# RMSNorm with row repetition: six of eight tiles compute their squares and sums four rows at a time

## The chip, the cores and the metric

The kernel runs on one core of a Trainium2 chip. The metric is the time of one execution on the device, in microseconds (us). The profile is of one such execution.

## The reference

```python
B, S, D = 8, 512, 2048
x_rep = np.repeat(x, 2, axis=1)
rms = np.sqrt((x_rep ** 2).mean(axis=-1, keepdims=True) + 1e-6)
out = (x_rep / rms * gamma[None, None, :]).astype(np.float32)
```

There are 4,096 rows of 2,048 float32 numbers. Each row is divided by its root mean square, multiplied by gamma, and written out twice, one copy after the other. 33.6 MB are read and 67.1 MB written.

## The kernel before

The rows are cut into eight tiles. A tile has 128 partitions with K = 4 rows each, so a load brings 4 MB and a store takes 8 MB. The buffer `y` of a tile has K * R = 8 row places in each partition, since each row is written twice (R = 2). The load puts the four input rows into places 4 to 7. `scale` for row k reads place 4 + k and writes the scaled row to place 2k, and `repeat` copies the even places to the odd ones. So the whole output tile is built in the buffer that held the input. The pool `rows` holds three such buffers: the load of tile i must wait until the store of tile i - 3 has landed.

The work of a tile, in `compute`, is row by row. ScalarE squares a row and sums it in the same instruction (`square`, L64, with an accumulator that a second, short instruction reads out), and takes the root of the mean (L68). The squared row itself is not used and goes to a scratch tile `sq` in PSUM. VectorE takes the reciprocal (L73) and multiplies the row by it and by gamma in one instruction (L74). After the four rows ScalarE copies places 0 and 2 to 1 and 3, and VectorE copies 4 and 6 to 5 and 7 (both L81, 128x4096).

The order on each engine is the program's own (`manual_schedule`): an engine takes its instructions in the order in which they are written, and waits at each until what it needs is there. On ScalarE the copy of tile i therefore stands ahead of the first square of tile i + 1.

All loads (L52) and stores (L56) of the tiles are issued from SP, and so go into one queue in one written order: loads 0 (in two halves), 1, 2; stores 0, 1, 2; loads 3, 4, 5; stores 3, 4; loads 6, 7; stores 5, 6, 7. A load or store that waits on SP holds back everything behind it. Gamma comes through ScalarE's queue (L95) and is spread over the partitions by GpSimd (L96) before the first scale.

```python
loads_after = {2: (3, 4, 5), 4: (6, 7)}
for i in range(ntiles):
    compute(i)
    store(i, 0, K)
    for j in loads_after.get(i, ()):
        load(j, nc.sync)
```

Of the kernel before, what the change touches and what calls it, by code (L numbers as in the profile page):

```python
# [1 line left out]

# [4 lines left out]


@with_exitstack
def kernel(  # L10
    ctx: ExitStack,
    tc: tile.TileContext,
    x: bass.AP,
    gamma: bass.AP,
    out: bass.AP,
):
    nc = tc.nc
    P = nc.NUM_PARTITIONS
    f32 = mybir.dt.float32
    Act = mybir.ActivationFunctionType  # L20
    Alu = mybir.AluOpType

    B, S, D = x.shape
    Bo, So, Do = out.shape
    R = So // S
    assert R == 2 and D == Do and B == Bo and So == S * R
    eps = 1e-6
    inv_d = 1.0 / float(D)


    K = 4
    N = B * S
    assert N % (P * K) == 0
    ntiles = N // (P * K)
    x_t = x.rearrange("b s d -> (b s) d").rearrange("(n p k) d -> n p k d", p=P, k=K)
    out_t = out.rearrange("b s d -> (b s) d").rearrange("(n p j) d -> n p (j d)", p=P, j=K * R)

    singles = ctx.enter_context(tc.tile_pool(name="singles", bufs=1))
    rows = ctx.enter_context(tc.tile_pool(name="rows", bufs=3))
    junk = ctx.enter_context(tc.tile_pool(name="junk", bufs=1, space=bass.MemoryType.PSUM))  # L40
    small = ctx.enter_context(tc.tile_pool(name="small", bufs=8))

    ys = []

    def load(i, eng, parts=1):


        y = rows.tile([P, K * R, D], f32, name="y")
        step = K // parts
        for k in range(0, K, step):  # L50
            at = K * (R - 1) + k
            eng.dma_start(out=y[:, at : at + step, :], in_=x_t[i, :, k : k + step, :])  # L52
        ys.append(y)

    def store(i, k0, k1):
        nc.sync.dma_start(  # L56
            out=out_t[i, :, R * k0 * D : R * k1 * D],
            in_=ys[i][:, R * k0 : R * k1, :].rearrange("p j d -> p (j d)"),
        )

    def square(i, k):
        sq = junk.tile([P, D], f32, name="sq")
        ss = small.tile([P, 1], f32, name="ss")
        nc.scalar.activation(  # L64
            out=sq[:], in_=ys[i][:, K * (R - 1) + k, :], func=Act.Square, accum_out=ss[:]
        )
        rms = small.tile([P, 1], f32, name="rms")
        nc.scalar.activation(out=rms[:], in_=ss[:], func=Act.Sqrt, scale=inv_d, bias=eps_t[:])  # L68
        return rms

    def scale(i, k, rms):
        rstd = small.tile([P, 1], f32, name="rstd")
        nc.vector.reciprocal(out=rstd[:], in_=rms[:])  # L73
        nc.vector.scalar_tensor_tensor(  # L74
            out=ys[i][:, R * k, :], in0=ys[i][:, K * (R - 1) + k, :], scalar=rstd[:], in1=gamma_b[:],
            op0=Alu.mult, op1=Alu.mult,
        )

    def repeat(i, k0, k1, copy):
        y_r = ys[i].rearrange("p (k r) d -> p k r d", r=R)  # L80
        copy(out=y_r[:, k0:k1, 1, :], in_=y_r[:, k0:k1, 0, :])  # L81

    def compute(i):
        for k in range(K):
            scale(i, k, square(i, k))
        repeat(i, 0, K // 2, nc.scalar.copy)
        repeat(i, K // 2, K, nc.vector.tensor_copy)


    ctx.enter_context(tc.manual_schedule())  # L90
    load(0, nc.sync, parts=2)
    gamma_b = singles.tile([P, D], f32, name="gamma_b")
    cuts = [0, *range(D // 4, D + 1, D // 8)]
    for c0, c1 in zip(cuts, cuts[1:]):
        nc.scalar.dma_start(out=gamma_b[0:1, c0:c1], in_=gamma[c0:c1].partition_broadcast(1))  # L95
    nc.gpsimd.partition_broadcast(out_ap=gamma_b[:], in_ap=gamma_b[0:1, :])  # L96
    eps_t = singles.tile([P, 1], f32, name="eps_t")
    nc.vector.memset(eps_t, eps)  # L98
    load(1, nc.sync)
    load(2, nc.sync)  # L100

    assert ntiles == 8
# [8 lines that stand above are left out]
# [1 line left out]
_INS = ['x', 'gamma']  # L114
_OUTS = [((8, 1024, 2048), 'float32')]


# [23 lines left out]
```

## Time and profile before

| | |
|---|---|
| median of 3 runs | 239.7 us (239.38 to 240.03) |
| the profiled execution's own time | 239.72 us |
| its span in the trace | 237.9 us |
| ScalarE busy | 101.0 us, 106 instructions |
| VectorE busy | 96.5 us, 73 instructions |
| bytes moved, mean rate over the span | 100.69 MB, 423 GB/s |

The own time is 1.8 us longer than the span, which begins and ends with the core's instructions. In the rows of the profile's costliest groups, a row gives the line, the engine, the operation, what is written and read, the number of instructions, then after the first bar the busy time of all of them in us and the mean of one in ns, and after the second bar how long the engine was idle just before them and what ended most of that. In the timeline a line gives the start in us, the length in us, and the instruction. A transfer has its issue in the timeline of SP (a third of a us); its data moves later, and its landing is seen where something that waited for it goes on.

### The profile page before, as it was taken

What the parts mean: (1) busy time and instruction counts of PE and PEld (TensorE: products, weight loads), DVE (VectorE), ACT (ScalarE), POOL (GpSimd) and SP (SyncE); (2) the same over time, 40 slices, a digit from 0 to 9 for tenths busy, and PEclk for the clock granted to TensorE, in tenths of its full rate; (3) what the DMA queues carried; (4) which work ended last, traced back from release to release, by engine and by line L of the source; (5) the groups of instructions that cost most, each with busy time, mean ns of one, the idle gap of its engine ahead of it and who ended that gap; (6) DMA issues with size and microseconds to landing.
All of it is one profiled execution on the core that took longest, in us unless ns stands there. A gap on an engine that the chain in (4) does not pass through costs nothing.

```text
span 237.9 us, 287 instructions
## 1 busy us (share of the span) xinstructions
DVE 96.5 (41%) x73; ACT 101.0 (42%) x106; POOL 2.5 (1%) x5
## 2 busy tenths in 40 slices
DVE  0049999960000000059999960000199990000000
ACT  2697999900000000099999920000599960000000
POOL 0030000000000000000000000000000000000000
DMA  7999998989899998999998999989998989999994
GB/s 265 436 446 441 441 441 353 530 353 496 386 452 430 397 485 353 441 441 441 441 518 364 464 419 430 452 369 430 435 518 364 518 364 485 397 452 430 408 474 176
DMA packets 2464, 100.69 MB, mean 423 GB/s; under 512 B 279, under 2 KB 285, under 8 KB 286
## 3 DMA queue, kind: packets, MB, share of 16 engines
q1 hardware_dynamic: 2448, 100.66, 98.5%
q14 instruction: 2, 0.02, 0.0%
q10 hardware_dynamic: 14, 0.01, 0.0%
HBM read 33.56 MB, written 67.11 MB: 423 GB/s over the span
## 4 chain that ended last, share of the span: by engine, by line
DMA 58%; ACT 12%; DVE 9%; issue 1%; POOLq 1%; ACTq 1%; SPq 0%
DMA y<-in_x_dram 33%; DMA out_dram<-y 21%; ACT sq L64 8%; DVE y L74 7%; DMA gamma_b<-in_gamma_dram 4%; ACT y L81 3%; DVE y L81 2%; ACT rms L68 1%; POOLq L136 1%; ACTq L95 1%; DVE rstd L73 0%; POOLq L96 0%; SPq L56 0%
## 5 line engine op out<-in xcount | busy, mean ns | idle before, releaser
L64 ACT ACTIVATE sq<-y 128x2048 f32<-128x2048 f32 x32 | 59.7, 1865 | 87.8 <-DMA y<-in_x_dram 87.8
L74 DVE SCALAR_TENSOR_TENSOR y<-y,rstd,gamma_b 128x2048 f32<-128x2048 f32 x32 | 75.3, 2352 | 4.1 <-POOL gamma_b L96 3.0
L73 DVE RECIPROCAL rstd<-rms 128x1 f32<-128x1 f32 x32 | 5.0, 158 | 94.6 <-ACT rms L68 94.3
L81 ACT COPY y<-y 128x4096 f32<-128x4096 f32 x8 | 28.7, 3590 | 1.4 <-DVE y L74 1.4
L81 DVE COPY y<-y 128x4096 f32<-128x4096 f32 x8 | 18.3, 2294 | 0.3
L68 ACT ACTIVATE rms<-ss,eps_t 128x1 f32<-128x1 f32 x32 | 9.4, 295 | 1.0
L64 ACT ACTIVATION_READ_ACCUMULATOR sq<-y 128x1 f32 x32 | 6.0, 187 | 0.0
L64 ACT ACT_TABLE_LOAD x1 | 1.3, 1283 | 3.0 <-issue 3.0
L96 POOL PARTITION_BROADCAST gamma_b<-gamma_b x1 | 2.3, 2294 | 12.2 <-DMA y<-in_x_dram 12.2
L68 ACT ACT_TABLE_LOAD x1 | 1.3, 1283 | 0.0
L98 DVE MEMSET eps_t<- 128x1 f32 x1 | 0.1, 59 | 0.8 <-PEq L125 0.8
L125 POOL MEMSET const-uint8-127<- 128x1 uint8 x1 | 0.1, 102 | 0.0
L125 POOL MEMSET const-bfloat16-1.0<- 128x1 bf16 x1 | 0.1, 101 | 0.0
L125 POOL MEMSET const-float32-0.0<- 128x1 f32 x1 | 0.1, 98 | 0.2 <-issue 0.2
L125 POOL MEMSET const-float32-1.0<- 128x1 f32 x1 | 0.1, 98 | 0.0
## 6 DMA issues: line engine op xcount, KB each, us to landing
y<-in_x_dram SPq DMA_DIRECT2D x7, 4096.0 KB, 14.6
y<-in_x_dram SPq DMA_DIRECT2D x2, 2048.0 KB, 7.4
out_dram<-y SPq DMA_DIRECT2D x8, 24.4
gamma_b<-in_gamma_dram ACTq DMA_DIRECT2D x6, 1.0 KB
gamma_b<-in_gamma_dram ACTq DMA_DIRECT2D x1, 2.0 KB
```

Of the source, the lines that this page charges most:

```text
L64: nc.scalar.activation(out=sq[:], in_=ys[i][:, K * (R - 1) + k, :], func=Act.Square, accum_out=ss[:])
L68: nc.scalar.activation(out=rms[:], in_=ss[:], func=Act.Sqrt, scale=inv_d, bias=eps_t[:])
L73: nc.vector.reciprocal(out=rstd[:], in_=rms[:])
L74: nc.vector.scalar_tensor_tensor(out=ys[i][:, R * k, :], in0=ys[i][:, K * (R - 1) + k, :], scalar=rstd[:], in1=gamma_b[:], op0=Alu.mult, o ...
L81: copy(out=y_r[:, k0:k1, 1, :], in_=y_r[:, k0:k1, 0, :])
L95: nc.scalar.dma_start(out=gamma_b[0:1, c0:c1], in_=gamma[c0:c1].partition_broadcast(1))
L96: nc.gpsimd.partition_broadcast(out_ap=gamma_b[:], in_ap=gamma_b[0:1, :])
L98: nc.vector.memset(eps_t, eps)
L125: nc = _bacc.Bacc("TRN2", target_bir_lowering=False, num_devices=1)
L136: with _tile.TileContext(nc) as tc:
```

## The change

Tiles 0 and 3, which the change's own words call tight, keep the work row by row. For tiles 1, 2, 4, 5, 6 and 7 the new function `scale_wide` squares all four rows in one ScalarE instruction of 128x8192. Its output goes to places 0 to 3 of the tile's own buffer. VectorE sums it with one `tensor_reduce` to four sums a partition; ScalarE takes the four roots in one instruction; VectorE takes the four reciprocals in one, and then scales row by row. `scale` no longer takes the reciprocal itself: for tiles 0 and 3 that instruction has moved into `compute`, just ahead of the call. `repeat`, the loads, the stores and their order stay as they were.

```diff
@@ -68,11 +68,9 @@
         nc.scalar.activation(out=rms[:], in_=ss[:], func=Act.Sqrt, scale=inv_d, bias=eps_t[:])
         return rms
 
-    def scale(i, k, rms):
-        rstd = small.tile([P, 1], f32, name="rstd")
-        nc.vector.reciprocal(out=rstd[:], in_=rms[:])
+    def scale(i, k, rstd):
         nc.vector.scalar_tensor_tensor(
-            out=ys[i][:, R * k, :], in0=ys[i][:, K * (R - 1) + k, :], scalar=rstd[:], in1=gamma_b[:],
+            out=ys[i][:, R * k, :], in0=ys[i][:, K * (R - 1) + k, :], scalar=rstd, in1=gamma_b[:],
             op0=Alu.mult, op1=Alu.mult,
         )
 
@@ -80,9 +78,29 @@
         y_r = ys[i].rearrange("p (k r) d -> p k r d", r=R)
         copy(out=y_r[:, k0:k1, 1, :], in_=y_r[:, k0:k1, 0, :])
 
+    def scale_wide(i):
+
+        nc.scalar.activation(out=ys[i][:, :K, :], in_=ys[i][:, K * (R - 1) :, :], func=Act.Square)
+        ss = small.tile([P, K], f32, name="ss_w")
+        nc.vector.tensor_reduce(
+            out=ss[:], in_=ys[i][:, :K, :], op=Alu.add, axis=mybir.AxisListType.X
+        )
+        rstd = small.tile([P, K], f32, name="rstd_w")
+        nc.scalar.activation(out=rstd[:], in_=ss[:], func=Act.Sqrt, scale=inv_d, bias=eps_t[:])
+        nc.vector.reciprocal(out=rstd[:], in_=rstd[:])
+        for k in range(K):
+            scale(i, k, rstd[:, k : k + 1])
+
     def compute(i):
-        for k in range(K):
-            scale(i, k, square(i, k))
+
+        if i in (0, 3):
+            for k in range(K):
+                rms = square(i, k)
+                rstd = small.tile([P, 1], f32, name="rstd")
+                nc.vector.reciprocal(out=rstd[:], in_=rms[:])
+                scale(i, k, rstd[:])
+        else:
+            scale_wide(i)
         repeat(i, 0, K // 2, nc.scalar.copy)
         repeat(i, K // 2, K, nc.vector.tensor_copy)
```

## The prediction

> **What bounds the kernel now.** I read the page first: busy share of the DMA engines, DMA queues, then the price rows.
>
> ```profile
> DMA  7999998989899998999998999989998989999994
> ...
> q1 hardware_dynamic: 2448, 100.66, 98.5%
> ...
> L64 ACT ACTIVATE sq<-y 128x2048 f32<-128x2048 f32 x32 | 59.7, 1865 | 87.8 <-DMA y<-in_x_dram 87.8
> L74 DVE SCALAR_TENSOR_TENSOR y<-y,rstd,gamma_b 128x2048 f32<-128x2048 f32 x32 | 75.3, 2352 | 4.1 <-POOL gamma_b L96 3.0
> L73 DVE RECIPROCAL rstd<-rms 128x1 f32<-128x1 f32 x32 | 5.0, 158 | 94.6 <-ACT rms L68 94.3
> L81 ACT COPY y<-y 128x4096 f32<-128x4096 f32 x8 | 28.7, 3590 | 1.4 <-DVE y L74 1.4
> L81 DVE COPY y<-y 128x4096 f32<-128x4096 f32 x8 | 18.3, 2294 | 0.3
> L68 ACT ACTIVATE rms<-ss,eps_t 128x1 f32<-128x1 f32 x32 | 9.4, 295 | 1.0
> ...
> y<-in_x_dram SPq DMA_DIRECT2D x2, 2048.0 KB, 7.4
> ```
>
> The one queue that moves x and out fills 98.5% of what 16 DMA engines have, and no slice between the ends falls below 8 tenths. ScalarE (101.0 us) and VectorE (96.5 us) are busy 40% of the span. So the end is set by transfers, and compute counts only where a store is issued too late to keep the queue filled. Both the margin and the loss are read from the issue times on SP (start, us, instruction):
>
> ```profile
> 27.05 0.35 SPq L56 DMA_DIRECT2D out_dram<-y  x1
> 39.22 0.34 SPq L56 DMA_DIRECT2D out_dram<-y  x1
> 51.39 0.33 SPq L56 DMA_DIRECT2D out_dram<-y  x1
> 52.84 0.34 SPq L52 DMA_DIRECT2D y<-in_x_dram  x1
> 72.14 0.34 SPq L52 DMA_DIRECT2D y<-in_x_dram  x1
> ...
> 115.86 0.34 SPq L56 DMA_DIRECT2D out_dram<-y  x1
> 128.25 0.34 SPq L56 DMA_DIRECT2D out_dram<-y  x1
> 140.24 0.34 SPq L52 DMA_DIRECT2D y<-in_x_dram  x1
> 159.63 0.34 SPq L52 DMA_DIRECT2D y<-in_x_dram  x1
> ...
> 184.02 0.34 SPq L56 DMA_DIRECT2D out_dram<-y  x1
> 196.41 0.33 SPq L56 DMA_DIRECT2D out_dram<-y  x1
> ```
>
> In order: stores 0, 1, 2, loads 3 and 4, stores 3 and 4, loads 6 and 7, stores 6 and 7. Load 3 waits for store 0 to land, load 4 for store 1, load 6 for store 3, load 7 for store 4, since each takes that tile's buffer. Their starts therefore time the landings: store 0 at 52.84, store 1 at 72.14, store 3 at 140.24, store 4 at 159.63. A store occupies the queue for 19.3 to 19.4 us. Load 6 lands at 169.3 (the ScalarE line below), 9.7 after store 4. Loads 7 and stores 5 and 6 follow without a gap: store 6 lands near 169.3 + 9.7 + 2 x 19.35 = 217.7, and one more store makes 237.1, 0.8 short of the span.
>
> Three ScalarE lines anchor the tiles: the first Square of tiles 1, 4 and 6.
>
> ```profile
> 23.28 1.88 ACT L64 ACTIVATE sq<-y 128x2048 f32<-128x2048 f32 x1
> ...
> 113.56 1.87 ACT L64 ACTIVATE sq<-y 128x2048 f32<-128x2048 f32 x1
> ...
> 169.34 1.88 ACT L64 ACTIVATE sq<-y 128x2048 f32<-128x2048 f32 x1 [30.91 <-DMA y<-in_x_dram]
> ```
>
> **The skill.** The Trainium skill, VectorE: DVE Perf Modes, "The perf-mode tier table", gives tensor_reduce only the 1x program, while a float32 copy in SBUF reaches 2x. The trace has no reduce; it agrees on the copy (2294 ns for 4096 elements, against 2352 for the 2048 of L74). ScalarE: Activation LUTs, "What ACT_TABLE_LOAD costs", states 186 ns + 0.833 ns an element; L81 on ScalarE gives 3590 where that makes 3598. DMA: Bandwidth & Descriptors, "Anatomy of one DMA", says that a semaphore wait sits on the issuing sequencer, ahead of dispatch. The trace agrees: load 3 goes out 1.45 us after store 2 and no load overtakes a store.
>
> **The change, part by part.** Tiles 1, 2, 4, 5, 6, 7 are wide.
> 1. ScalarE loses 24 rows of Square with accumulator read and 24 Sqrt of 128x1, 24 x (1.865 + 0.187 + 0.295) = 56.3 us (the 187 ns is the read's own row). It gains six Squares of 128x8192 at 0.186 + 8192 x 0.000833 = 7.0 us and six Sqrt at 0.3: 43.8. It was never the bound, so these 12.5 us are worth nothing in themselves. The new target, rows 0 to 3 of the tile, is in a buffer that the load has already waited for.
> 2. VectorE loses 18 reciprocals (2.8 us) and gains six reduces of 128x8192. At 1x, with the 2048-element slope of the copy row (2294 ns for 4096 elements at 2x, about 2133 of it streaming and 160 fixed), a reduce is 8192 x 2133/2048 + 160 = 8.7 us. No row shows it. From below, a 2x program would make it 4.4; from above, the L74 row per element (2352/2048) makes 9.4. I take 8.7. VectorE comes to 96.5 - 2.8 + 52.2 = 146 us, still below the transfers.
> 3. What was a pipeline becomes a series. Before, Square of row k+1 ran beside the scale of row k. Now the reduce waits for the whole Square. Sqrt waits for the reduce, and behind it on ScalarE stand this tile's copy and the next tile's Square. From the Square's start: 7.0 Square, 8.7 reduce, 0.3 Sqrt, 0.16 reciprocal, some 0.1 in handoffs (0.03 each in the chain of waits), so the first scale starts at 16.3. Two scales end at 20.9, four at 25.7, the VectorE copy at 28.0, and SP issues the store at **28.1**. Tile 4 needed 128.25 - 113.56 = 14.7 before, tile 1 15.9. The ScalarE copy starts at 20.95 and ends at 24.55; the overlap seen before (23.28 against 19.77 + 3.60) lets the next Square start at **24.5**. Two wide tiles in a row thus issue stores 24.5 us apart, while the queue empties one in 19.35.
> 4. The other edits cost nothing: the reciprocal moved out of scale() for tiles 0 and 3 keeps its place in VectorE's order, and the unused PSUM scratch is off every wait. DMAs keep number, size and order.
>
> The stores' dates (L is the time from issue on an empty queue until data flows at the full rate):
> - Tile 1: 23.28 + 28.1 = 51.4; the queue runs dry at 52.84, so a gap of at most L - 1.4.
> - Tile 2: 23.28 + 24.5 + 28.1 = 75.9; its turn came at 72.14. Gap 3.7 + L, any gap of tile 1 included. Loads 3, 4 and 5 stand behind this store on SP. All then moves by this amount; tile 3's own margin stays, 120.6 (101.2 + 2 x 9.7) less 115.86.
> - Tile 4: 113.56 + 28.1 = 141.7 against 140.24, both shifted alike. Gap 1.4 + L. Loads 6 and 7 are behind it.
> - Tile 5: about 24.5 later, 166.2 against load 7's 179.0 (169.3 + 9.7). No gap.
> - Tile 6: 169.34 + 28.1 = 197.4 against 198.4 (179.0 + 19.35): at most L - 1.0, and taken up by the next.
> - Tile 7: 169.34 + 24.5 + 28.1 = 221.9 against 217.7. Gap 4.2 + L, nothing after it but its own 19.35.
>
> The sum is 9.3 + 3L. The trace has no store into an empty queue; the nearest is the first load. It was issued at 0.72, its first bytes appear between 1.5 and 2.0 in the windows, and the 2 MB that should take 4.85 (half of 9.7) landed in 7.4. So L lies between 0.8 and 2.5. I take the middle, **1.7**: part of the load's slow start is a cold queue. That gives 9.3 + 5.1 = 14.4 us on the profiled 239.72 us (span 237.9), hence **254 us**; the profiled run is the median of 239.7 within 0.02.
>
> **Rivals.**
> A (the series outlasts the queue, as above): for it, the margins by the same lines. Tile 2 could be 72.14 - 51.39 = 20.8 us later and gets 24.5; tile 7 could be 21.3 later and gets 25.5; tile 4 12.0 and gets 13.4.
> B (the reduce is quick enough to stay hidden): with a 4.4 us reduce the three dates fall by 8.6, 4.3 and 8.6 us, more than 3.7 + L, 1.4 + L and 4.2 + L at L = 1.7. Nothing is left: 239.7 us. The point of decision is the reduce's price: (8.7 - r) must exceed 1.4 + 1.7 for tile 4 and half of 5.9 for tile 7, so r below 5.6 us. Against it stands the skill's 1x.
> C (the reduce costs 9.4 like L74's pace): its price enters twice in tile 2, once in 4, twice in 7: 5 x 0.7 = 3.5 us more, 257.6.
> D (restarting the queue is dearer than any load showed, L = 4): 9.3 + 12 = 21.3, 261 us.
> No case gives a gain: the queue was full, the first store is still tile 0's and unchanged.
>
> **How the numbers follow.** A at 0.75, C 0.13, D 0.05, B 0.04, and 0.03 for what I don't foresee, a third of it a gain. A's own ends are L of 0.8 and 2.5: 11.7 and 16.8 us, 251.4 and 256.5. The range takes 0.5 us off the first for shorter handoffs and adds C to the far end: 250.5 to 258.5. A measurement here can tell about 0.3% from no change: faster 0.01, same 0.04, slower 0.95.
>
> **What would show it.** In the changed profile: reduce rows near 8.7 us and Squares of 7.0; stores 2, 4 and 7 issued near 75.9, 147.1 (141.7 + 5.4) and 230.4 (221.9 + 5.4 + 3.1); DMA slices dipping at three places (about 72 to 78, 146 to 149, 226 to 232) and a share of the queue near 93%. A reduce under 5.6 us, or DMA slices as full as now, would make it wrong, as would a store that goes out before its four scales end.

## The result and the profile after

The changed kernel takes **255.29 us** (median of 5, 255.25 to 255.42) against 239.5 us for the kernel before on the same chips. The ratio is 1.0657, with a 95% interval of 1.0643 to 1.0672: 15.8 us slower. The forecast was 254.0, in a range of 250.5 to 258.5. The profiled execution took 255.31 us with a span of 253.5, which is 15.6 more than before.

The page of the changed kernel: busy shares, the slices of the DMA engines with the rate under them, the queue, and the rows of the new instructions.

```profile
DVE 146.6 (58%) x61; ACT 92.5 (36%) x46; POOL 2.5 (1%) x5
...
DMA  7999997999909998999999779799999797973977
GB/s 285 461 414 414 414 486 341 496 403 424 496 0 496 403 424 331 460 445 419 372 455 496 331 331 496 331 352 465 424 414 496 332 498 331 496 331 165 496 331 331
...
q1 hardware_dynamic: 2448, 100.66, 94.0%
...
L85 DVE TENSOR_REDUCE ss_w<-y 128x4 f32<-128x8192 f32 x6 | 52.1, 8686 | 33.4 <-ACT y L83 33.4
...
L83 ACT ACTIVATE y<-y 128x8192 f32<-128x8192 f32 x6 | 42.2, 7028 | 10.3 <-DMA y<-in_x_dram 10.3
...
L89 ACT ACTIVATE rstd_w<-ss_w,eps_t 128x4 f32<-128x4 f32 x6 | 1.8, 298 | 52.5 <-DVE ss_w L85 52.5
```

The same bytes go over the same queue, but its share fell from 98.5% to 94.0%. A slice is 253.5/40 = 6.3 us here, and a packet of a transfer is counted in the slice in which it begins. In the twelfth, from about 70 to 76 us, none begins (those begun before it end by 71.9), and the thirty-seventh, from 228 to 234, shows a 3. Neither engine is near full: VectorE, with 50 us more than before, stands at 58%. The two long idle times at the ends of the last rows name the series: each reduce waits for a Square, and each root waits 8.75 us for a reduce.

SP's issue times (start, us, instruction):

```profile
51.15 0.34 SPq L56 DMA_DIRECT2D out_dram<-y  x1
75.69 0.33 SPq L56 DMA_DIRECT2D out_dram<-y  x1
...
97.45 0.33 SPq L52 DMA_DIRECT2D y<-in_x_dram  x1
...
147.59 0.34 SPq L56 DMA_DIRECT2D out_dram<-y  x1
...
169.33 0.34 SPq L52 DMA_DIRECT2D y<-in_x_dram  x1
...
207.42 0.34 SPq L56 DMA_DIRECT2D out_dram<-y  x1
231.96 0.33 SPq L56 DMA_DIRECT2D out_dram<-y  x1
```

These are stores 1 and 2, load 5 (which waits for store 2 to land), store 4, load 7 (which waits for store 4), stores 6 and 7. Store 2 went out at 75.69, after its turn at about 72.1. Load 5 followed at 97.45, 5.9 us later than the 91.56 of before; load 7 at 169.33, 9.7 later; and the span ends 15.6 later. So the loss comes in three pieces, 5.9, 3.8 and 5.9 us, one for each late store: 2, 4 and 7.

The chain of work that ended last goes through compute there (start, us, what):

```profile
44.19 3.61 ACT y L79
47.80 6.94 ACT y L83
...
54.76 8.70 DVE ss_w L85
...
63.48 0.31 ACT rstd_w L89
...
64.03 6.89 DVE y L72 x3
...
73.33 2.30 DVE y L79
...
75.69 0.33 SPq L56
```

Tile 1's copy (L79) holds tile 2's Square on ScalarE until 47.8. Then Square, reduce, root, scales, copy and store follow, each waiting for the whole of the one before. Before the change this stretch of the chain was a transfer.

### The profile page after: what moved, and what is told of

Read it like the earlier page. It is cut to its first block, busy times and chain, and to the rows that moved or that the text cites. A ratio compares the mean times of both kernels' runs of the same rounds, so it can differ in the third digit from the quotient of the medians.

```text
span 253.5 us, 221 instructions
## 1 busy us (share of the span) xinstructions
DVE 146.6 (58%) x61; ACT 92.5 (36%) x46; POOL 2.5 (1%) x5
## 4 chain that ended last, share of the span: by engine, by line
DVE 37%; DMA 28%; ACT 21%; issue 3%; POOLq 1%; ACTq 1%; SPq 0%
DMA y<-in_x_dram 25%; DVE ss_w L85 17%; DVE y L72 16%; ACT y L83 14%; DMA gamma_b<-in_gamma_dram 4%; ACT y L79 3%; ACT sq L64 3%; DVE y L79 3%; POOLq L154 1%; ACTq L113 1%; ACT rstd_w L89 1%; DVE rstd_w L90 0%; ACT rms L68 0%; SPq L56 0%; DVE rstd L100 0%
## 5 line engine op out<-in xcount | busy, mean ns | idle before, releaser
L85 DVE TENSOR_REDUCE ss_w<-y 128x4 f32<-128x8192 f32 x6 | 52.1, 8686 | 33.4 <-ACT y L83 33.4
L72 DVE SCALAR_TENSOR_TENSOR y<-y,rstd_w,gamma_b 128x2048 f32<-128x2048 f32 x24 | 55.4, 2350 | 0.7 <-DVE rstd_w L90 0.3
L83 ACT ACTIVATE y<-y 128x8192 f32<-128x8192 f32 x6 | 42.2, 7028 | 10.3 <-DMA y<-in_x_dram 10.3
L79 ACT COPY y<-y 128x4096 f32<-128x4096 f32 x8 | 28.8, 3605 | 31.4 <-DVE y L72 31.4
L64 ACT ACTIVATE sq<-y 128x2048 f32<-128x2048 f32 x8 | 14.9, 1868 | 38.3 <-DMA y<-in_x_dram 38.3
L100 DVE RECIPROCAL rstd<-rms 128x1 f32<-128x1 f32 x8 | 1.3, 158 | 44.7 <-ACT rms L68 44.7
L89 ACT ACTIVATE rstd_w<-ss_w,eps_t 128x4 f32<-128x4 f32 x6 | 1.8, 298 | 52.5 <-DVE ss_w L85 52.5
L72 DVE SCALAR_TENSOR_TENSOR y<-y,rstd,gamma_b 128x2048 f32<-128x2048 f32 x8 | 18.8, 2352 | 3.2 <-POOL gamma_b L114 3.0
L79 DVE COPY y<-y 128x4096 f32<-128x4096 f32 x8 | 18.3, 2294 | 0.3
L68 ACT ACTIVATE rms<-ss,eps_t 128x1 f32<-128x1 f32 x8 | 2.4, 296 | 0.2
L90 DVE RECIPROCAL rstd_w<-rstd_w 128x4 f32<-128x4 f32 x6 | 1.1, 178 | 2.2 <-ACT rstd_w L89 2.2
L64 ACT ACTIVATION_READ_ACCUMULATOR sq<-y 128x1 f32 x8 | 1.5, 187 | 0.0
```

The lines of the kernel that those rows point to most:

```text
L64: nc.scalar.activation(out=sq[:], in_=ys[i][:, K * (R - 1) + k, :], func=Act.Square, accum_out=ss[:])
L72: nc.vector.scalar_tensor_tensor(out=ys[i][:, R * k, :], in0=ys[i][:, K * (R - 1) + k, :], scalar=rstd, in1=gamma_b[:], op0=Alu.mult, op1= ...
L83: nc.scalar.activation(out=ys[i][:, :K, :], in_=ys[i][:, K * (R - 1) :, :], func=Act.Square)
L85: nc.vector.tensor_reduce(out=ss[:], in_=ys[i][:, :K, :], op=Alu.add, axis=mybir.AxisListType.X)
L89: nc.scalar.activation(out=rstd[:], in_=ss[:], func=Act.Sqrt, scale=inv_d, bias=eps_t[:])
L90: nc.vector.reciprocal(out=rstd[:], in_=rstd[:])
```

## The experiments

One explanation is set against four rivals. **A**: a store misses its turn in the queue because a wide tile is a series. The rivals say that something else costs: **E** the added traffic, **F** VectorE's added work, **G** another part of the change, **H** the transfer rate. A store's lead is the time by which its issue comes ahead of the landing of the transfer before it in the queue. The condition of each kernel is edited in the line `if i in (0, 3):` unless a diff says otherwise. Each difference is from the kernel before on the same chip.

### Two wide tiles, apart and in a row

```diff
-        if i in (0, 3):
+        if i not in (1, 5):
```

> Only tiles 1 and 5 are wide, the other six go row by row. Theory A (a wide tile costs time only where its store misses its turn in the queue): tile 1's store goes out near 51.2 with store 0 landing near 52.9, tile 5's has over 10 us of margin, so no change: 239.5 us, within 1 us. Rival E (the added VectorE and ScalarE traffic in SBUF slows the transfers, so each wide tile costs 15.8/6 = 2.6 us wherever it stands): 244.8 us, with stores taking longer than 19.3 us beside a reduce.

Measured: 242.14 us (ratio 1.0093, 1.0077 to 1.011), 2.6 us slower. Neither A (no change) nor E (5.3 us) had it. The issue times on SP (store 1, load 5, load 6):

```profile
51.31 0.34 SPq L56 DMA_DIRECT2D out_dram<-y  x1
...
92.46 0.33 SPq L52 DMA_DIRECT2D y<-in_x_dram  x1
...
142.56 0.34 SPq L52 DMA_DIRECT2D y<-in_x_dram  x1
```

Load 5 is 0.9 us behind its date of before and load 6 2.3 behind (142.56 against 140.24). Something was lost though no store was issued after its turn.

```diff
-        if i in (0, 3):
+        if i not in (1, 2):
```

> Only tiles 1 and 2 are wide: as many wide tiles as in the run with 1 and 5. Theory A: store 2 goes out near 75.7 and misses its turn, 5.9 us as in the changed kernel: 245.4 us. If the small losses after the gap (loads 5 and 7 and the stores behind them, 1.5 us in the changed kernel) come from the restart, up to 1.5 us more, 246.9. Rival E (traffic): 244.8 us, the same as with tiles 1 and 5.

Measured: 246.35 us (1.028, 1.0266 to 1.0294), 6.8 us slower, inside A's 245.4 to 246.9. The same number of wide tiles costs 4.2 us more when they follow each other, which speaks for A against E. Store 2, load 5 and load 6:

```profile
75.63 0.33 SPq L56 DMA_DIRECT2D out_dram<-y  x1
...
97.40 0.33 SPq L52 DMA_DIRECT2D y<-in_x_dram  x1
...
147.13 0.34 SPq L52 DMA_DIRECT2D y<-in_x_dram  x1
```

From store 2's issue to load 5 it is 21.77 us, where a store holds the queue for 19.3. And from load 5 to load 6 it is 49.73, against 140.24 - 91.56 = 48.68 before: 1.05 us more in a stretch in which no store was late.

### One wide tile with margin

```diff
-        if i in (0, 3):
+        if i != 5:
```

> Only tile 5 is wide; its store has more than 10 us of margin behind load 7. The run with tiles 1 and 5 wide lost 2.6 us where none was expected. Theory A2 (tile 1's store, 1.3 us ahead of store 0's landing, was already too late for part of the queue): with tile 1 row by row again nothing is lost, 239.5 us within 0.5. Rival E (each wide tile's traffic costs, 1.3 us a tile by that run): 240.8 us.

Measured: 239.7 us, ratio 1.0004 (0.9994 to 1.0013): no change. The reduce (8.7 us) ran beside transfers as in the changed kernel, so E is out. The trace also records each packet that a DMA engine moves (a store is 8 packets of 64 KB on each of 16 engines), and this agrees: the packets of the changed kernel's store 1, beside which tile 2's Square and reduce run, took 2.42 to 2.46 us, against 2.42 before the change. The 2.6 us of tiles 1 and 5 belong to tile 1, whose store was issued about 1.3 us ahead of store 0's landing.

### The same sums, row by row

(Abridged: the bodies of the two helpers are left out, and comments stand for them.)

```diff
+        def square_row(k):   # Square of row k to place 1 + 2 * (k % 2)
+        def sum_row(k):      # tensor_reduce of that place, then Sqrt
+        square_row(0)
+        square_row(1)
+        sum_row(0)
         for k in range(K):
+            if k + 1 < K:
+                sum_row(k + 1)
+            if k + 2 < K:
+                square_row(k + 2)
+            rstd = small.tile([P, 1], f32, name="rstd_w")
+            nc.vector.reciprocal(out=rstd[:], in_=root[k][:])
+            scale(i, k, rstd[:])
```

> The six tiles again sum on VectorE (four reduces of 128x2048 a tile), but row by row: Square of one row, its reduce, root, reciprocal and scale, the next row's Square meanwhile; the Square goes to the free odd places of the tile. VectorE has the work of the changed kernel and 18 reduces and 18 reciprocals more in number. Theory A (the series of whole-tile instructions makes the stores late): a tile takes about 23.7 us from its first Square to its store, pairs are 21.6 apart, store 2 near 70.4 against 72.1, store 7 near 214.7 against 217.7: 239.5 us, at most 2 more. Rival F (the sums' move to VectorE costs, in whatever order): VectorE is as busy as in the changed kernel (147 us or more), so about 255 us.

Measured: 239.91 us, ratio 1.0012 (1.0002 to 1.0022), 0.3 us over before. Its page:

```profile
DVE 148.9 (63%) x97; ACT 98.8 (42%) x82; POOL 2.5 (1%) x5
...
L91 DVE TENSOR_REDUCE ss_w<-y 128x1 f32<-128x2048 f32 x24 | 54.2, 2278 | 13.7 <-ACT y L85 13.7
```

VectorE is busier than in the changed kernel (148.9 against 146.6 us), and the time is nearly that of before. Moving the sums to VectorE is not what costs; doing four rows at once is. F is out. Store 2 went out here at 68.90, 3.0 us ahead of store 1's landing (load 4 at 71.94), and nothing was lost by it: load 5 followed at 91.48, against 91.56 before.

### A shorter reduce

```diff
-            out=ss[:], in_=ys[i][:, :K, :], op=Alu.add, ...
+            out=ss[:], in_=ys[i][:, :K, : D // 2], op=Alu.add, ...
```

> The changed kernel with the reduce over the first half of each squared row only (the other half of each sum is left out). The reduce should take 8192/2 elements, 4.4 us. Theory A, with the point of decision at a reduce of 5.6 us: stores 2, 4 and 7 are 8.5, 4.3 and 8.5 us earlier and all in time: 239.5 to 240.5 us. Rival G (the gaps come from the wide Square or from the order on ScalarE, not from the reduce): most of the 15.8 us stays, 250 us or more.

Measured: 241.7 us (1.0084, 1.0069 to 1.01). Of the 15.8 us 13.6 went with the 4.3 us of each reduce, so G, by which most would stay, is out. The reduce is one link of the series; the next experiment moves another. But 2.2 us stayed that A did not expect. Store 4 and load 6 (which marks store 3's landing):

```profile
137.11 0.34 SPq L56 DMA_DIRECT2D out_dram<-y  x1
139.78 0.34 SPq L52 DMA_DIRECT2D y<-in_x_dram  x1
```

Store 4 went out 2.7 us ahead of the landing, by A in good time.

### The next Square ahead of the copy

```diff
             scale_wide(i)
+        if i in (1, 4, 6):
+            square_wide(i + 1)
         repeat(i, 0, K // 2, nc.scalar.copy)
```

(`scale_wide` leaves out the Square for tiles 2, 5 and 7.)

> The changed kernel with one move on ScalarE: in the pairs 1-2, 4-5 and 6-7 the second tile's wide Square goes ahead of the first tile's copy. Theory A: the second tile's reduce then follows the first tile's VectorE copy at once, VectorE sets the distance of two stores (8.7 + 0.5 + 9.3 + 2.3 = 20.8 us instead of 24.5), so store 2 goes out near 72.0 instead of 75.7 and store 7 3.7 us earlier as well; tile 4 stays. About 7.4 us less than the changed kernel: 248 us, between 247 and 249. Rival G (the order on ScalarE does not matter, VectorE's 146 us do): 255 us.

Measured: 247.7 us (1.0346, 1.033 to 1.0362), as A had it. Stores 2 and 7:

```profile
71.90 0.33 SPq L56 DMA_DIRECT2D out_dram<-y  x1
...
224.36 0.33 SPq L56 DMA_DIRECT2D out_dram<-y  x1
```

Store 2 is 3.8 us earlier than in the changed kernel, with nothing shortened: only the copy no longer stands ahead of the Square.

### Something to fill the gap

```diff
-    loads_after = {2: (3, 4, 5), 4: (6, 7)}
+    loads_after = {1: (3,), 2: (4, 5), 4: (6, 7)}
```

> The changed kernel with load 3 issued ahead of store 2 on SP, nothing else moved. Its buffer is free at 52.9, so it can fill the queue while store 2 is late. Theory A: load 3 moves 9.7 us from 72.3 on, store 2 (75.7) is in time behind it, the 5.9 us gap of tile 2 goes; load 4 lands near 111 and store 4 goes out near 139 against store 3's landing at 140.2, so tile 4's 3.1 us shrink to between 0.5 and 1.5; tile 7's 4.8 stay: 245 to 248 us. Rival H (the loss is a matter of rate, not of an empty queue): 255 us.

Measured: 249.25 us (1.0409, 1.039 to 1.0427), 6.0 us less than the changed kernel but above A's 248. Store 1, load 3, store 2, load 5, and then store 4 and load 6:

```profile
51.13 0.34 SPq L56 DMA_DIRECT2D out_dram<-y  x1
52.63 0.34 SPq L52 DMA_DIRECT2D y<-in_x_dram  x1
75.67 0.33 SPq L56 DMA_DIRECT2D out_dram<-y  x1
...
103.82 0.34 SPq L52 DMA_DIRECT2D y<-in_x_dram  x1
...
141.56 0.34 SPq L56 DMA_DIRECT2D out_dram<-y  x1
142.59 0.34 SPq L52 DMA_DIRECT2D y<-in_x_dram  x1
```

Filling the gap works: store 2 is as late as ever and the time falls, where H allowed no gain. But store 2 landed at 103.8, where 72.3 + 9.7 + 19.3 = 101.3 was expected: 2.5 us went though store 1 was issued 1.5 us ahead of store 0's landing (52.63). By the packet records the engines were idle there for 0.1 us on average; the rest went in the last packets of store 1 and of load 3. Store 4 then had a lead of only 1.0 us.

### A restart that was to have nothing behind it

```diff
+        if i == 2:
...
+            for j in (5, 3, 4):
+                fill(j, new[j - 3], nc.sync)
```

(Tiles 1 and 2 wide; load 5 first among the three behind store 2. `fill` is the DMA of `load`, and `new` holds the three new buffers.)

> Tiles 1 and 2 wide, and behind store 2 the first load on SP is load 5, which cannot go out until store 2 has landed: store 2 runs with nothing behind it. With loads 3 and 4 behind it, it took 21.8 us from issue to landing, 2.4 more than its 19.3; the changed kernel's last store, with nothing behind it, 20.8. Theory L1 (a load issued 0.4 us behind a store slows its start): 20.8 us. Theory L2 (a restart takes 2.4 us, the last store is an exception): 21.8 us. Its total time is not compared: other gaps open, as load 5 goes out on an empty queue and load 3 lands later.

Measured: 253.67 us (1.0596, 1.0576 to 1.0615). Store 2 and the loads behind it:

```profile
75.71 0.33 SPq L57 DMA_DIRECT2D out_dram<-y  x1
76.15 1.33 SPq L49 DMA_DIRECT2D y<-in_x_dram  x2
...
97.47 0.33 SPq L49 DMA_DIRECT2D y<-in_x_dram  x1
```

The run did not do what it was meant to do. Two loads went out at once behind store 2, the first 0.44 us after it, and only the third waited until store 2 had landed. So store 2 had loads behind it as before, and its 21.76 us cannot choose between L1 and L2.

The packet records of the traces say more. In the changed kernel the first packets of store 2 began 0.83 us after its issue, and those of the last store, with nothing behind it, 0.83 us too: the loads behind a store do not slow its start, so L1 is out. The first seven packets of each engine took 2.4 to 2.5 us in both. The eighth took 2.8 to 3.6 us in store 2, where load 3's first packets follow, and 2.42 in the last store. So the last packet of store 2 ended 21.39 us after its issue, and that of the last store 20.38. The last stores of the two runs before this one also ended 20.38 and 20.37 us after their issue. The 1.0 us between the two kinds of restart thus lies at the end of the store, where another transfer follows. Why it is lost there was not shown.

### How early is early enough

Only tile 4 is wide, and the length of its reduce sets the store's date. First the full reduce:

```diff
-        if i in (0, 3):
+        if i != 4:
```

> Only tile 4 is wide. By the runs so far a store must be issued 2.4 us ahead of the last landing or the queue loses the difference, and after such a loss the next change from loads to stores loses another 1.0 us. Tile 4's store goes out near 141.5, 1.4 us after store 3 has landed. Rule R: 1.4 + 2.4 = 3.8, with 1.0 at load 7: 4.8 us over before, 244.3 us. Rule S (only the empty time and the 1.7 us of the forecast count): 3.1 us, 242.6.

Measured: 244.29 us (1.0203, 1.0188 to 1.0218): rule R's 244.3.

```diff
-            out=ss[:], in_=ys[i][:, :K, :], op=Alu.add, ...
+            out=ss[:], in_=ys[i][:, :K, : 6 * D // 8], op=Alu.add, ...
```

> As with tile 4 alone wide, but its reduce takes 6 eighths of each squared row (the rest of the sum is left out), about 6.5 us. The store goes out 2.2 us earlier, near 139.4, 0.8 ahead of store 3's landing. Rule R: 1.6 + 1.0 = 2.6 us over before, 242.1. Rule S: 0.9 us, 240.4.

Measured: 242.04 us (1.0108, 1.0093 to 1.0123): R again. With `: D // 2` and `: 3 * D // 8` in the same place:

> As before it, with 4 eighths of each squared row in tile 4's reduce, 4.4 us (half of the sum is left out). The store goes out near 137.3, 2.9 ahead of store 3's landing. Rule R: nothing lost, 239.5. Rule R2 (the lead must be over 3 us, as the run with six halved reduces suggests, where 2.7 us ahead lost 2.2): 1 to 2.2 us over, 240.5 to 241.7. Rule S: 239.5.

> As before it, with 3 eighths of each squared row in tile 4's reduce, 3.4 us (the rest of the sum is left out). The store goes out near 136.2, 4.0 ahead of store 3's landing. Rules R, R2 and S: nothing lost, 239.5 us; anything over 240.2 would mean that a wide tile costs in tile 4's place whatever its store's date.

Measured: 241.89 us (1.0107, 1.0091 to 1.0124) and 239.44 us (1.0001, 0.9992 to 1.0009). The first is above the rules R, R2 (by 0.2 us) and S, the second is no change. Their reduce rows, and store 4 with load 6 in each, the half first:

```profile
L85 DVE TENSOR_REDUCE ss_w<-y 128x4 f32<-128x4096 f32 x1 | 4.4, 4420 | 4.8 <-ACT y L83 4.8
...
137.29 0.34 SPq L56 DMA_DIRECT2D out_dram<-y  x1
140.01 0.34 SPq L52 DMA_DIRECT2D y<-in_x_dram  x1
```

```profile
L85 DVE TENSOR_REDUCE ss_w<-y 128x4 f32<-128x3072 f32 x1 | 3.4, 3354 | 4.8 <-ACT y L83 4.8
...
136.16 0.34 SPq L56 DMA_DIRECT2D out_dram<-y  x1
139.93 0.34 SPq L52 DMA_DIRECT2D y<-in_x_dram  x1
```

| reduce of tile 4 | store 4's lead on store 3's landing | time over before |
|---|---|---|
| 8.7 us | 1.4 us late (141.65 against 140.24) | 4.9 us |
| 6.6 us | 0.5 us (139.36, load 6 at 139.88) | 2.6 us |
| 4.4 us | 2.7 us | 2.5 us |
| 3.4 us | 3.8 us | 0.0 us |

The loss is not R's straight line. It is nearly the same at leads of 0.5 and 2.7 us, and gone at 3.8. The packet records show two kinds. At a lead of 0.5 us the engines stood idle for 1.2 us on average ahead of store 4: its first packets began at 140.20, when those of store 3 had ended by 139.39. At 2.7 us they were idle for 0.01 us, so the queue did not run dry. There the loss lies at the changes between stores and loads that follow: a little where load 6 comes behind store 4, and most at the end of load 7, ahead of store 5, where packets took up to 2.5 us instead of 1.21. With a lead of 3.8 us load 7 ended at 178.62, with 2.7 at 180.79. At load 7's issue nothing was missing yet (159.65, before 159.63). Why these changes cost after one store and not after another stays open.

## Why the prediction was right

**Bound and mechanism: right, and shown.** The queue sets the end, and compute costs only through the stores' dates. The same work with margin costs nothing (tile 5 alone), the same VectorE time row by row costs nearly nothing, and the next Square's place on ScalarE alone moves 7.6 us. The section of the Trainium skill that the prediction names for semaphore waits (DMA: Bandwidth & Descriptors, "Anatomy of one DMA") describes DMAs that GpSimd issues. For SP's queue the traces decide, and they agree: load 5 went out at 97.45, 0.4 us after store 2's last packet.

**Prices: right.** The reduce took 8686 ns (8.7 forecast), at 1x as the Trainium skill says (VectorE: DVE Perf Modes, "The perf-mode tier table"): from 4420 ns for 4096 elements to 8686 for 8192 it is 1.04 ns an element. The Square took 7.03 (7.0), the root 0.30, the reciprocals 0.18. Tile 1's store went out 51.15 - 23.16 = 28.0 us after its first Square (28.1), and stores 1 and 2 are 24.54 apart (24.5). ScalarE's total was 92.5, not the 88.5 that the step gives: it subtracted row sums, and rows overlap. Nothing hangs on it.

**The three gaps: right in place, and the term that was mis-sized is L.** I took 1.7 us for a restart. Store 2 took 97.45 - 75.69 = 21.76 us to load 5's issue and store 4 169.33 - 147.59 = 21.74 to load 7's, so L was 2.4 twice, at the upper end of the bound; from store 7 to the end it was 253.5 - 231.96 = 21.5, less 19.35 and the 0.8 of the tail: 1.4. The account: 14.4 forecast, + 0.7 and + 0.7 for L at tiles 2 and 4, - 0.3 at tile 7, - 0.2 because store 2 went out at 75.7 and not 75.9, + 0.2 because store 7 came 231.96 - 179.13 = 52.8 us behind tile 6's Square and not 52.6. That is 15.5 of the 15.6 measured; the rest is rounding and tile 4's date. What L is made of I had wrong. I called it the time from issue until data flows, and by the packet records that is 0.83 us. The rest of the 2.4 is the 0.4 us between a store's last packet and the landing from which I counted, and the 1.2 us by which the store's packets took longer than in a full queue, most of it at its end. That 1.7 was near their sum is in part luck.

**Rival B's point of decision: wrong.** I held that a reduce under 5.6 us would leave nothing. At 4.4 us 2.2 us were left, and with tile 4 alone 2.5. Two terms were missing in it. A store needs a longer lead than L: at 2.7 us time was still lost, though the queue did not run dry, and at 3.8 it was not. And a late or nearly late store costs again at the next change from loads to stores, the 1.05 us between loads 5 and 6 with tiles 1 and 2 wide. In the changed kernel neither shows in the total, since each of these falls into the next gap, where the queue waits for compute anyway. That is why a sum without them came within 1.3 us; the forecast had not reckoned with this, so it was luck.

**Tile 1's "gap of at most L - 1.4": it exists, and was indeed taken up.** With tiles 1 and 5 wide there was no gap at tile 2 to take it up, and it cost 2.6 us with what followed. The engines were idle ahead of store 1 for only 0.2 us of this on average, by the packet records; the rest went at the changes behind store 2 and behind load 5.

## What to carry to other kernels

When transfers fill the span, price an edit in dates: for each store, when its turn in the queue comes and when its last instruction ends, through every wide tile in a row, since what fits once may not fit twice (24.5 us a tile against 19.35 a store). One instruction over four rows saves instructions and loses the overlap between rows; the row-by-row form with the same sums on VectorE kept the time. And check the lead of a transfer that must follow without a gap against what a restart costs, not against zero: here leads of 3.0 us (store 2, row by row) and 3.8 us (store 4) lost nothing, and 2.7 us (store 4) lost 2.5.

## What was not expected of the hardware

- A queue that ran dry cost 2.4 us at its restart in five kernels' stores in mid-run (21.7 to 21.8 us from issue to the load that waited for it, against 19.3). The changed kernel's last store needed only 1.4. The difference of 1.0 us between it and store 2 lies in the last packets of store 2, which had a load behind it. Why it arises there stays open.
- A store issued 2.7 us ahead of the landing before it, so into a queue that did not run dry, still cost 2.5 us in all, at the later changes between stores and loads. In the runs without a loss such changes cost almost nothing (about 0.1 us a packet at most, on average over the engines), with one exception: the first, from load 2 to store 0, cost 0.9 to 1.4 us in every run, before the change too (there load 2 took 10.7 us from its first packets to its last, loads 3 to 5 9.7). The cause stays open.
